# A hybrid decoder block on one core: smaller tiles in the RWKV solve, fewer rows zeroed, another owner of the gating, the dynamic loop moved

## The chip, the cores and the metric

One Trainium2 chip, of which the program uses one core. The metric is the device time of one execution in microseconds (us). The kernel before took 2051.95 us (median of three runs, 2043.92 to 2052.5).

## What is computed

The reference is one decoder layer on 256 tokens of width 2048, in float32:

```python
xn   = rmsnorm(x)
proj = xn @ W_in
attn = moba_attention(proj[..., :A], ...)
rw   = rwkv7_time_mix(token_shift_lerp(proj[..., 3*A:], mu), ...)
h    = x + concat([attn, rw]) @ W_out
h    = h + peer_ffn(rmsnorm(h))
out  = rmsnorm(h, final_g)
```

The attention has 8 heads of 128, all tokens in one block. RWKV has 16 heads of 64, whose state is carried over the tokens. `peer_ffn` scores 128 x 128 product keys for 8 heads, each token keeps the 16 best experts of each head, and the output is the sum over them of `gate * gelu(x . u[e]) * v[e]`, where expert e is one row of `u` and one row of `v` (2048 wide, 16384 rows).

## The kernel before, in words

**Gemms.** Every weight comes in halves of 128x1024 floats (`prefetch`, L191; the load is L197, on SP's queue). ACT rounds a half to a high part (`whi`, L204), DVE subtracts to get the low part (`wlo`, L205), and three matmuls make one product: high x high, high weight x low input, low weight x high input (L218 to L220). In PEER's `gemm_wide` (L234) it is one matmul 512 wide (L240) and one 256 wide (L242) for each of the 16 tiles of the depth; a step of `hidden` is 128 experts, and there are 128 steps.

**Input projection.** `products` (L639) multiplies 8 units of RWKV pairs of heads (r, k, v), then 8 units of attention heads (q, k, v). Each finished unit becomes a generator in `live`; while the next units' matmuls are issued, `deal` and `step_all` step up to four of these generators after every fourth tile. `rwkv` works in 4 chunks of 64 tokens (`NC` = 4). For each chunk it inverts a triangular 64x64 matrix for both heads of the pair at once, as a 128x128 tile with two blocks on the diagonal, in 5 levels of two products (`pw`, L496, and `px`, L502). `clear` (L633) issues the DMAs that zero `rows_d`, a table in HBM with one row of 257 floats per expert: 23 DMAs of 1028 KB (L637), two per pair of RWKV heads and one per attention head until all are issued.

**PEER.** `choose` finds the best 16 keys per tile of 128 tokens, `table` builds the gate table of that tile in HBM (`gate_d`), `hidden` multiplies `u` and takes the gelu on ACT (`gelu`, L1122, from `part`, which DVE adds at L1138). `places` (L1005) gives every chosen expert a row of `rows_d`: first 28 blocks of 128 rows for those that only tile 0 chose, 28 for tile 1 alone, and then a middle part, for those of both tiles and what did not fit before. Experts that nobody chose get a row number past the table, which is written too but never read. `scatter` (L1098) takes step after step of `hidden`: `gated` (L1080) multiplies gate and gelu into an `at` section (on POOL), and an indirect DMA (L1107, issued by POOL) writes its 128 rows to their places. One gate table of 1024 KB (`gt`, L1075, loaded by POOL's queue) serves eight sections, one `at` tile holds seven. `choose`, `table` and `scatter` run beside `hidden`: `run` (L1156) gives each a credit per fourth tile and takes off what each `yield` says that it costs.

**V.** After the last step, blocks of 128 rows of `rows_d` are read back (L1200), the rows of `v` that they name are gathered (an indirect DMA, L1205), split, and multiplied: 28 blocks for tile 0 only, 28 for tile 1 only, `MID` = 52 for both. Reads run five blocks ahead of the matmuls. After all of them, a loop whose count is computed on the chip, `tc.For_i(MID, count)` (L1264), multiplies what the middle part holds beyond 52 blocks. Then the residual is added (L1295), normed, and written (L1286).

With the inputs of the runs the choices need 50.3 blocks of 128 rows in the middle part, worked out from the reference, so `count` is 51: the loop has no iteration, before and after.

```python
        for c in range(NC):
            nc.tensor.matmul(o4(pw)[:, c], M[:, c, 0:128], lo_(X)[:, c], start=(c == 0), ...)
        nc.vector.tensor_tensor(lo_(wm), o4(pw), lo_(lv(i)...), op=ALU.mult)
        yield
```

Of the kernel before, what the change touches and what calls it, by code (L numbers as in the profile page):

```python
# [10 lines left out]
F32 = mybir.dt.float32  # L11
# [51 lines left out]
C0, C1, MID, DN = 28, 28, 52, 2  # L63
B1, BM = C0 * 128, (C0 + C1) * 128
BT = BM + 128 * 128
# [3 lines left out]
def consts():  # L69
# [6 lines left out]
    c[:, K_MSK:K_MSK + P] = same & (p[:, None] < p[None])  # L76
# [3 lines left out]
    for i in range(6):  # L80
        n = 1 << i
        lv = (p[:, None] // (2 * n) == p[None] // (2 * n)) & (p[:, None] % (2 * n) >= n) & (p[None] % (2 * n) < n)
        c[:, K_LV + i * P:K_LV + (i + 1) * P] = lv
        if i == 0:
            c[:, K_M1T:K_M1T + P] = lv.T
# [69 lines left out]
def block_kernel(ctx: ExitStack, tc: tile.TileContext, x, cols, consts, w_lora, w_gate, w_rkv, w_qkv,  # L155
# [13 lines left out]
    rows_d = dp.tile([BT + NEXP, ROW], F32, name="rows_d")  # L169
# [11 lines left out]
    for w, n in ((w_gate, 2), (w_rkv, 3 * RJ), (w_qkv, 3 * AH)):  # L181
        halves += [(w[m, i].rearrange("p k c -> p (k c)"), HK * P) for m in range(n) for i in range(2)]
# [163 lines left out]
    wms = [p1.tile([P, NC, P], F32, name=f"wm{i}") for i in range(1, 6)]  # L346
# [8 lines left out]
    mska = kc(K_MSK, 128).rearrange("p (h t) -> p h t", h=2).unsqueeze(1).to_broadcast([P, 2, 2, CH])  # L355
    mskr = kc(K_MSK + 128, 192).unsqueeze(1).to_broadcast([P, 2, 192])
# [3 lines left out]
    idb = ident.unsqueeze(1).to_broadcast([P, NC, 128])  # L360
# [15 lines left out]
    def rwkv(j, r, k, vv):  # L376
# [82 lines left out]
        for q in range(0, NC, 2):  # L459
            pc = bank("pc", [P, 4, 128])  # L460
            for c in range(2):
                for i, src in enumerate((nbd, kbd)):
                    nc.tensor.matmul(pc[:, 2 * c + i, :], src[:, q + c, :], ar[:, q + c, :],
                                     start=c + i == 0, stop=c + i == 2, skip_group_check=True)
            pc2 = pc.rearrange("p (c i) n -> p c (i n)", c=2)
            nc.vector.tensor_tensor(M[:, q:q + 2, 0:128].rearrange("p a (h t) -> p a h t", h=2),
                                    pc2[:, :, 0:CH].unsqueeze(2).to_broadcast([P, 2, 2, CH]), mska, op=ALU.mult)
            nc.vector.tensor_tensor(M[:, q:q + 2, 128:320], pc2[:, :, CH:], mskr, op=ALU.mult)
            yield

# [13 lines left out]
        for i in range(1, 6):  # L484
            n = 1 << i
            nblk = P // (2 * n)
# [13 lines left out]
            px = bank("px", [P, NC, CH])  # L500
            for c in range(NC):
                nc.tensor.matmul(o4(px)[:, c], wm[:, c, :], hi_(XT)[:, c], start=(c == 0), stop=(c == NC - 1),  # L502
                                 skip_group_check=True)
            nc.vector.tensor_tensor(hi_(XT), hi_(XT), o4(px), op=ALU.add)
            yield

        y = tmp("y", "y")[:, :S]
        Z = None
        for c in range(NC):
# [15 lines left out]
            nc.tensor.matmul(sa_p, XT[:, c, :], r0, start=True, stop=True)  # L525
# [104 lines left out]
    gv = rows_d[0:BT].rearrange("(p f) o -> p f o", p=P)  # L630
    zero = []

    def clear(n):  # L633
        for _ in range(n):
            i = len(zero)
            if i < BT // P // 8:
                zero.append(nc.sync.dma_start(gv[:, 8 * i:8 * i + 8, :], zt.unsqueeze(1).to_broadcast([P, 8, ROW])))  # L637

    def products():  # L639
# [18 lines left out]
        for j in range(RJ):  # L658
            while len(live) > 4:
                step_all()  # L660
# [11 lines left out]
            clear(2)  # L672
        state["pools"] = [spl]
        for h in range(AH):
            while len(live) > 4:
                step_all()
# [8 lines left out]
            clear(1)  # L685

# [236 lines left out]
    def table(t):  # L923


        while t not in chosen:
            yield 0
# [73 lines left out]
    place = cp.tile([P, P], I32, name="place")  # L1001
    eint = sp.tile([P, P], I32, name="eint")
    nblk = cp.tile([P, 1], I32, name="nblk")

    def places():  # L1005
# [12 lines left out]
        off = sp.tile([P, 4], F32, name="off")  # L1018
# [22 lines left out]
        V.scalar_tensor_tensor(pos, mid, -1.0, enum, op0=ALU.mult, op1=ALU.mult)  # L1041
        V.scalar_tensor_tensor(tmp_, mid, -float(BT), pos, op0=ALU.mult, op1=ALU.add)
        V.scalar_tensor_tensor(pos, enum, float(BT), tmp_, op0=ALU.add, op1=ALU.add)
        yield 1.2
        for t, n, base in ((0, C0, 0), (1, C1, B1)):
# [3 lines left out]
            V.scalar_tensor_tensor(tmp_, rank[t], float(base), inside[t], op0=ALU.add, op1=ALU.mult)  # L1049
            V.tensor_tensor(pos, pos, tmp_, op=ALU.add)  # L1050
# [3 lines left out]
        ps = ranks((2, 1))  # L1054
        yield 0.5
        V.tensor_copy(off[:, 2:4], ps[:, :, 0])
        V.scalar_tensor_tensor(rank[2], sums[2], off[:, 2:3], mid, op0=ALU.add, op1=ALU.subtract)
        V.scalar_tensor_tensor(tmp_, rank[2], float(BM), mid, op0=ALU.add, op1=ALU.mult)
        V.tensor_tensor(pos, pos, tmp_, op=ALU.add)
        V.tensor_copy(place, pos)  # L1060

        V.tensor_scalar(off[:, 3:4], off[:, 3:4], 127.0, None, op0=ALU.add)
        V.tensor_copy(nblk, off[:, 3:4])
        V.tensor_scalar(nblk, nblk, 7, None, op0=ALU.logical_shift_right)
        V.tensor_copy(eint, enum)
        chosen["places"] = True
# [13 lines left out]
    def gated(i2, eng=nc.gpsimd):  # L1080

        if i2 % 7 == 0:
            rows[0] = big("at")
            n = min(7, NKEY - i2)
            eng.tensor_copy(rows[0][:, 0:n * ROW].rearrange("p (n c) -> p n c", c=ROW)[:, :, T].bitcast(I32),
                                  eint[:, i2:i2 + n])
# [9 lines left out]
        return at  # L1096

    def scatter():  # L1098
        while "places" not in chosen:
            yield 0  # L1100
        gates_of(0)
        yield 0
        for i2 in range(NKEY - DN):
            while hid["n"] <= i2:
                yield 0
            at = gated(i2)
            s_ = nc.gpsimd.indirect_dma_start(  # L1107
                out=rows_d, out_offset=bass.IndirectOffsetOnAxis(ap=place[:, i2:i2 + 1], axis=0),
                in_=at, in_offset=None)
            for z_ in done:  # L1110
                tc.declare_no_dep(s_.ins, z_.ins, reason="other rows")
            for z_ in zero:
                tc.add_manual_dep(s_.ins, z_.ins.name, SYNC, reason="zeros first")
            done.append(s_)
            yield 1.5
# [38 lines left out]
    beside = [[both_choices(), 0.55, 0.0], [tables(), 0.38, 0.0], [scatter(), 1.0, 0.0]]  # L1154
# [67 lines left out]
    for i2 in range(NKEY - DN, NKEY):  # L1222
        with tc.issue_after(state["gelu"].ins), tc.issue_after(u_end.ins):
            ah, al_ = halves_of(gated(i2, nc.vector)[:, 0:T])
# [18 lines left out]
    for k in range(len(order) + 5):  # L1243
# [18 lines left out]
    count = nc.values_load(nblk[0:1, 0:1], min_val=0, max_val=128,  # L1262
                           skip_runtime_bounds_check_because="a count of at most 16384 experts in blocks of 128")
# [59 lines left out]
```

## Time and profile before

| what | value |
|---|---|
| runs | 2043.92, 2051.95, 2052.5 us |
| profiled execution: its own time / its span | 2048.21 / 2046.3 us |
| PE, DVE, ACT, POOL busy | 95%, 70%, 52%, 35% |
| mean granted TensorE clock | 0.98 |
| DMA | 444 MB, 217 GB/s over the span |

The span runs from the first to the last record; 1.9 us of the execution lie around it. PE is the busiest engine; its row in the 40 slices of the page shows 90% or more everywhere but in the first four slices, the 26th to 28th, the 31st and the last. A busy PE at a granted clock of 1.0 works at 2.4 GHz, at 0.5 at 1.2 GHz.

The names of engines in the rows: PE is TensorE, PEldq its sequencer for weight loads, DVE VectorE, ACT ScalarE, POOL GpSimd, SP SyncE.

### The profile page before, as it was taken

The page shows a single profiled execution, that of the slowest core. Times are in us where ns is not written, and L with a number is a line of the kernel's source. Part 1 is how long each engine was busy: PE and PEld are TensorE (multiplying, and loading weights), DVE is VectorE, ACT ScalarE, POOL GpSimd, SP SyncE. Part 2 cuts the span into 40 slices and gives each one's busy share as a digit, 9 for nine tenths or more (in the row PEclk, how much of TensorE's full clock was granted, in tenths as well). Part 3 has the DMA queues.
Part 4 walks back from the last instruction along what each step waited for, and adds up shares of the span by engine and source line. Part 5 has one row for each costly group of instructions (what it writes and reads, how often), then busy time and mean ns, then how long its engine had stood idle before and what let it go on. Part 6 is the DMA issues. An engine that isn't in the chain of part 4 may idle for free. (4 is left out here: it accounts for less than half of the span.)

```text
span 2046.3 us, 31447 instructions
## 1 busy us (share of the span) xinstructions
PE 1935.7 (95%) x11804; PEld 1723.3 (84%) x11804; DVE 1437.7 (70%) x2090; ACT 1062.9 (52%) x1696; POOL 712.1 (35%) x654
## 2 busy tenths in 40 slices
PE   7888999999999999999999999887998999999996
PEld 6788999999879998878888888776887788888885
DVE  6766878766556888999878866544755666666665
ACT  4534554345455444677676744433444555555554
POOL 7211211100000000023424269998986333333322
PEclk9999999999999999999999999998999999999998
DMA  8999322225576666556666678786888887878783
GB/s 248 258 247 246 98 87 87 88 83 146 190 227 198 184 180 188 173 175 197 215 195 217 196 237 264 248 267 229 270 267 271 343 284 280 296 286 293 281 297 141
DMA packets 135291, 443.91 MB, mean 217 GB/s; under 512 B 14369, under 2 KB 52257, under 8 KB 118497
## 3 DMA queue, kind: packets, MB, share of 16 engines
q1 hardware_dynamic: 106992, 289.24, 47.7%
q0 software_dynamic: 28144, 152.65, 20.4%
q8 instruction: 93, 1.52, 0.3%
q14 instruction: 62, 0.50, 0.1%
HBM read 380.07 MB, written 61.76 MB: 216 GB/s over the span
## 5 line engine op out<-in xcount | busy, mean ns | idle before, releaser
L205 DVE TENSOR_TENSOR wlo<-raw,whi 128x1024 fp32r<-128x1024 f32 (+1 forms) x408 | 569.6, 1402 | 301.1 <-ACT whi L204 291.9
L240 PE MATMUL ps_gm<-nx,whi 128*128 128x512 f32 x2048 | 731.8, 400 | 24.9 <-ACT whi L204 21.9
L204 ACT ACTIVATE whi<-raw 128x1024 fp32r<-128x1024 f32 (+1 forms) x408 | 429.5, 1055 | 384.2 <-issue 89.5
L242 PE MATMUL ps_gm<-nx,wlo 128*128 128x256 f32 x2048 | 579.4, 283 | 14.2 <-DVE wlo L205 14.2
L240 PEld LDWEIGHTS ps_gm<-nx,whi 128*128 128x128 f32 x2048 | 387.8, 189 | 112.6 <-ACT whi L204 22.6
L242 PEld LDWEIGHTS ps_gm<-nx,wlo 128*128 128x128 f32 x2048 | 390.3, 191 | 20.1 <-DVE wlo L205 19.7
L249 DVE TENSOR_TENSOR vlo<-vraw,vhi 128x2048 fp32r<-128x2048 f32 x108 | 247.9, 2297 | 151.6 <-ACT vhi L248 146.1
L248 ACT ACTIVATE vhi<-vraw 128x2048 fp32r<-128x2048 f32 x108 | 205.9, 1913 | 156.3 <-DVE vlo L249 146.8
L1205 POOL DMA_INDIRECT vraw<-in_v_dram,ag x108 | 145.1, 1343 | 294.8 <-PE ps_gm L1194 210.0
L218 PE MATMUL ps_gm<-xh,whi 128*128 128x256 f32 x640 | 192.7, 301 | 0.8 <-ACT whi L204 0.8
L220 PE MATMUL ps_gm<-xh,wlo 128*128 128x256 f32 x640 | 185.1, 289 | 3.2 <-DVE wlo L205 3.1
L219 PE MATMUL ps_gm<-xl,whi 128*128 128x256 f32 x640 | 185.6, 290 | 0.0
L1107 POOL DMA_INDIRECT rows_d<-at,place x126 | 169.5, 1345 | 36.9 <-POOL at L1093 15.8
L951 POOL TENSOR_TENSOR mt<-gc 128x1024 f32<-128x1024 f32 x16 | 39.7, 2482 | 345.5 <-ACT gc L979 345.5
L1122 ACT ACTIVATE A<-part 128x256 f32<-128x256 f32 x128 | 53.1, 415 | 166.7 <-DVE part L1138 131.3
L1093 POOL TENSOR_TENSOR at<-A,gt 128x256 f32<-128x256 f32 x126 | 129.2, 1041 | 5.4 <-DMA gt<-gate_d 3.6
L220 PEld LDWEIGHTS ps_gm<-xh,wlo 128*128 128x128 f32 x640 | 122.8, 192 | 4.6 <-DVE wlo L205 4.2
L218 PEld LDWEIGHTS ps_gm<-xh,whi 128*128 128x128 f32 x640 | 122.9, 192 | 1.9 <-ACT whi L204 1.2
L219 PEld LDWEIGHTS ps_gm<-xl,whi 128*128 128x128 f32 x640 | 122.9, 192 | 0.7
L807 POOL DMA_DIRECT2D skb<-in_sk_dram x16 | 8.6, 540 | 250.7 <-ACT mh L248 167.7
L945 ACT ACTIVATE ob<-ob,pick 128x128 f32<-128x128 f32 x256 | 83.9, 390 | 19.6 <-DVE ob L937 19.6
L373 POOL TENSOR_TENSOR df<-ext 128x256 f32<-128x256 f32 (+1 forms) x28 | 23.8, 850 | 155.3 <-DVE ext L371 142.4
(1521 smaller groups left out, 3925.5 us busy)
## 6 DMA issues: line engine op xcount, KB each, us to landing
raw<-in_u_dram SPq DMA_DIRECT2D x256, 512.0 KB, 4.1
raw<-in_w_rkv_dram SPq DMA_DIRECT2D x48, 512.0 KB, 7.3
raw<-in_w_qkv_dram SPq DMA_DIRECT2D x48, 512.0 KB, 3.6
rows_d<-zt SPq DMA_DIRECT2D x23, 1028.0 KB, 15.8
raw<-in_w_out_dram SPq DMA_DIRECT2D x32, 512.0 KB, 3.9
raw<-in_wq_dram SPq DMA_DIRECT2D x32, 512.0 KB, 3.6
gate_d<-gc SPq DMA_DIRECT2D x16, 1024.0 KB, 6.5
gt<-gate_d POOLq DMA_DIRECT2D x16, 1024.0 KB, 9.0
```

The lines of the kernel that those rows point to most:

```text
L204: nc.scalar.activation(hi[:, :n], raw[:, :n], AF.Copy)
L205: state["dve"] = nc.vector.tensor_tensor(lo[:, :n], raw[:, :n], hi[:, :n].bitcast(F32), op=ALU.subtract)
L218: nc.tensor.matmul(ps, a, xh(kt), start=first and k == 0, stop=False)
L219: nc.tensor.matmul(ps, a, xl(kt), start=False, stop=False)
L220: state["mm"] = nc.tensor.matmul(ps, b, xh(kt), start=False, stop=last and k == HK - 1)
L240: nc.tensor.matmul(ps.rearrange("p z t -> p (z t)"), hi[:, k * P:(k + 1) * P], x_.rearrange("p z t -> p (z t)"), start=i + k == 0, stop=Fa ...
L242: state["mm"] = nc.tensor.matmul(ps[:, 0, :], lo[:, k * P:(k + 1) * P], x_[:, 0, :], start=False, stop=i == 1 and k == HK - 1, skip_group_ ...
L248: nc.scalar.activation(hi, src, AF.Copy)
L249: nc.vector.tensor_tensor(lo, src, hi.bitcast(F32), op=ALU.subtract)
L1093: eng.tensor_tensor(at[:, 0:T].rearrange("p (q t) -> p q t", q=KT), As[i2 // 8][:, k, :].rearrange("p (q t) -> p q t", q=KT), g.rearrange( ...
L1107: s_ = nc.gpsimd.indirect_dma_start(out=rows_d, out_offset=bass.IndirectOffsetOnAxis(ap=place[:, i2:i2 + 1], axis=0), in_=at, in_offset=None)
L1205: nc.gpsimd.indirect_dma_start(out=raw, out_offset=None, in_=vf, in_offset=bass.IndirectOffsetOnAxis(ap=ag[:, T:ROW].bitcast(I32), axis=0))
```

## The change

Six things, in the order of the diff.

1. `MID` 52 to 51; experts that nobody chose get rows behind the middle part, numbered by another rank in `places`; one row tile of zeros is scattered behind them (`behind`, `zr`), so that the last block read of the middle part holds only sound rows. So only the one-tile sections (`BM` rows) are zeroed beforehand: 7 DMAs of 1028 KB in place of 23, one per unit (`clear(1)`).
2. The units are taken in the order r0, r1, r2, a0, r3, a1, ... in place of eight pairs and then eight heads.
3. The solve holds each head's 64x64 matrix by itself: tiles `X`, `XT`, `wm` are half as wide, each product is two matmuls 64x32 per chunk, one per half of the partitions, and one copy per pair (`bd`, on POOL) makes the 128x128 tile that the later product reads.
4. `table` waits until both tiles have chosen; the credits are 0.6 and 0.45 for 0.55 and 0.38.
5. `gated` works on DVE in place of POOL; a section costs the credit 2.0, not 1.5.
6. The loop stands in the sequence of blocks, after step 40, and its blocks end no sum.

```diff
-C0, C1, MID, DN = 28, 28, 52, 2
+C0, C1, MID, DN = 28, 28, 51, 2
-BT = BM + 128 * 128
+BT = BM + (NKEY - DN + 1) * 128
...
+    ORDER = [("r", 0), ("r", 1)] + [x for j in range(2, RJ) for x in (("r", j), ("a", j - 2))] + [("a", AH - 2), ("a", AH - 1)]
...
-            X = W("X", [P, NC, 128], XB)
+            X = W("X", [P, NC, CH], XB)
             nc.vector.transpose(X.rearrange("p c s -> p (c s)"), XT.rearrange("p c s -> p (c s)"))
-            pw = bank("pw", [P, NC, CH])
+            pw = bank("pw", [P, NC, CH // 2])
             for c in range(NC):
-                nc.tensor.matmul(o4(pw)[:, c], M[:, c, 0:128], lo_(X)[:, c], start=(c == 0), stop=(c == NC - 1),
-                                 skip_group_check=True)
+                for hs in both:
+                    nc.tensor.matmul(o4(pw)[hs, c], M[hs, c, 64:128], lo_(X)[hs, c], start=True, stop=True,
+                                     skip_group_check=True)
...
+        XB_ = W("XB", [P, NC, 128], 2)
+        bd(XB_, XT)
...
-            nc.tensor.matmul(sa_p, XT[:, c, :], r0, start=True, stop=True)
+            nc.tensor.matmul(sa_p, XB_[:, c, :], r0, start=True, stop=True)
...
-    gv = rows_d[0:BT].rearrange("(p f) o -> p f o", p=P)
+    gv = rows_d[0:BM].rearrange("(p f) o -> p f o", p=P)
...
-            clear(2)
+            clear(1)
...
-        while t not in chosen:
+        while 0 not in chosen or 1 not in chosen:
...
-    def gated(i2, eng=nc.gpsimd):
+    def gated(i2):
...
-        eng.tensor_tensor(at[:, 0:T].rearrange("p (q t) -> p q t", q=KT),
+        nc.vector.tensor_tensor(at[:, 0:T].rearrange("p (q t) -> p q t", q=KT),
...
+        zr = big("zr")[:, 0:ROW]
+        nc.gpsimd.memset(zr, 0.0)
+        into_rows(zr, behind)
         yield 0
         for i2 in range(NKEY - DN):
             while hid["n"] <= i2:
                 yield 0
             at = gated(i2)
...
-            yield 1.5
+            into_rows(at, place[:, i2:i2 + 1])
+            yield 2.0
...
-    beside = [[both_choices(), 0.55, 0.0], [tables(), 0.38, 0.0], [scatter(), 1.0, 0.0]]
+    beside = [[both_choices(), 0.6, 0.0], [tables(), 0.45, 0.0], [scatter(), 1.0, 0.0]]
...
-    with tc.For_i(MID, count, 1) as i:
-        ag, _ = rows_at(i * P + BM)
-        block((0, 1), *divided(ag, gather(ag)), True)
+        if k == 40:
...
+            with tc.For_i(MID, count, 1) as i:
+                rows[2] = rows[1]
+                ag, _ = rows_at(i * P + BM)
+                rows[1] = rows[2]
+                block((0, 1), *divided(ag, gather(ag)), False)
```

How this moves the instructions is seen at two places. The first is PE's own order in the input projection, around one `pw` product of a solve; gemm is L218 to L220 before and L224 to L226 now, the product L496 and now L502. Before:

```order
L218 MATMUL ps_gm<-xh,whi 128x256
L219 MATMUL ps_gm<-xl,whi 128x256
L220 MATMUL ps_gm<-xh,wlo 128x256
L525 MATMUL ps_ch<-r_1369,XT 128x128
L496 MATMUL ps_pw<-X,M 128x64 x4
L392 MATMUL ps_mm<-lor,l_1377 128x256
L218 MATMUL ps_gm<-xh,whi 128x256
```

Now:

```order
L224 MATMUL ps_gm<-xh,whi 128x256
L225 MATMUL ps_gm<-xl,whi 128x256
L226 MATMUL ps_gm<-xh,wlo 128x256
L557 MATMUL ps_mm<-y,bo_198 128x256
L502 MATMUL ps_pw<-X,M 64x32 x8
L224 MATMUL ps_gm<-xh,whi 128x256
L225 MATMUL ps_gm<-xl,whi 128x256
```

Four products with both heads in one tile became eight with one head each, and each run of eight stands alone between products of 128 rows; there are 80 such runs (8 pairs x 5 levels x 2). In float32 each row of the order is two matmuls in the trace.

The second place is the scatter stage, on POOL, which issues the scatters (`rows_d`) and the loads of the gate tables (`gt`). Before:

```order
L1107 DMA rows_d<-at,place 39936x257 x2
L1075 DMA gt_13178<-gate_d 128x16x128
L1093 TENSOR_TENSOR at<-A_8687,gt_13060 128x256 x2
L1107 DMA rows_d<-at,place 39936x257 x2
L1093 TENSOR_TENSOR at<-A_8687,gt_13060 128x256 x2
L1107 DMA rows_d<-at,place 39936x257 x2
L1093 TENSOR_TENSOR at<-A_8687,gt_13060 128x256
```

POOL now:

```order
L1127 DMA rows_d<-at,place 23424x257 x4
L1103 DMA gt_13934<-gate_d 128x16x128
L1127 DMA rows_d<-at,place 23424x257 x12
L1103 DMA gt_14093<-gate_d 128x16x128
L1127 DMA rows_d<-at,place 23424x257 x8
L1103 DMA gt_14241<-gate_d 128x16x128
```

And DVE now, at the same sections, with the waits of each instruction; `wlo` (L211) is the low half of the weights of `hidden`, `DMASW` a queue of POOL's DMAs:

```order
L211 TENSOR_TENSOR wlo<-raw,whi 128x1024 [waits DMAHW6_49,PE_49,Activation_49]
L1171 TENSOR_TENSOR part<-part,ps_gm 128x256 [waits Activation_49]
L1121 TENSOR_TENSOR at<-A_10407,gt_13934 128x256 [waits DVE_49]
L1121 TENSOR_TENSOR at<-A_10407,gt_13934 128x256 x3
L211 TENSOR_TENSOR wlo<-raw,whi 128x1024 [waits DMAHW7_49,PE_49,Activation_49]
L1121 TENSOR_TENSOR at<-A_10992,gt_14093 128x256 [waits DMASW7_49]
L1121 TENSOR_TENSOR at<-A_10992,gt_14093 128x256
L211 TENSOR_TENSOR wlo<-raw,whi 128x1024 [waits DMAHW0_49,PE_49,Activation_49]
```

The multiplication by the gates has left POOL's order, whose loads of gate tables now stand among the scatters alone; on DVE it stands between the halves of the weights, and its first section of a table waits for that table's load.

## Rows read from the trace of the kernel before

**Rows 1.** Windows: length, then busy us (x) of PE, PEld, DVE, ACT, POOL, clock, DMA, GB/s.

```profile
80.00:205.00 125.00, 109.61 (x855) 106.04 (x854) 88.05 (x163) 51.47 (x88) 23.75 (x39) 0.96 1.03 243
205.00:500.00 295.00, 290.62 (x2344) 281.34 (x2343) 222.02 (x448) 140.80 (x271) 37.26 (x46) 1.00 0.32 95
...
850.00:950.00 100.00, 91.79 (x559) 80.40 (x558) 99.38 (x164) 69.35 (x144) 22.94 (x14) 1.00 0.56 175
...
1230.00:1560.00 330.00, 299.11 (x1665) 257.93 (x1664) 190.97 (x155) 139.32 (x208) 298.07 (x267) 0.96 0.79 257
...
1600.00:2029.00 429.00, 429.00 (x1894) 355.06 (x1892) 274.19 (x210) 231.55 (x208) 137.54 (x101) 1.00 0.78 280
```

**Rows 2.** Waits of ACT, 80 to 200 us: us in total, times, longest.

```profile
ACT whi L204 <- DMA raw<-in_w_rkv_dram: 25.6, 3, 14.1
```

**Rows 3.** DMAs issued, 80 to 200 us: KB each, median us to landing.

```profile
rows_d<-zt SPq DMA_DIRECT2D x16, 1028.0 KB, 16.8
raw<-in_w_rkv_dram SPq DMA_DIRECT2D x21, 512.0 KB, 11.5
```

**Rows 4.** Groups by line and form, PE, 0 to 520 us: busy, mean ns, idle before.

```profile
L496 PE MATMUL ps_pw<-X,M 128*128 128x64 f32 x320 | 40.9, 269 | 1.7 <-DVE X L493 1.6
```

**Rows 5.** Timeline of PE around one product of the solve: start, duration, instruction.

```profile
246.70 1.00 PE L496 MATMUL ps_pw<-X,M 128*128 128x64 f32 x8
247.52 0.36 PE L218 MATMUL ps_gm<-xh,ml 128*128 128x256 f32 x1
247.72 0.28 PE L219 MATMUL ps_gm<-xl,ml 128*128 128x256 f32 x1
247.84 0.28 PE L220 MATMUL ps_gm<-xh,ml 128*128 128x256 f32 x1
```

**Rows 6.** Timeline of PE just after an idle stretch, products two columns wide.

```profile
1201.01 0.58 PE L1033 MATMUL ps_pc<-tot,we 128*128 128x2 f32 x2 [3.50 <-DVE tot L1027]
1201.45 0.57 PE L1034 MATMUL ps_pc<-tot,kb 128*128 128x2 f32 x2
```

**Rows 7.** Windows: the microsecond in which these products start, columns as in rows 1.

```profile
1201.00:1202.00 1.00, 0.99 (x5) 1.00 (x5) 0.49 (x3) 0.00 (x0) 0.29 (x2) 0.50 0.92 295
```

**Rows 8.** Timeline of DVE in the scatter stage.

```profile
1222.47 1.23 DVE L205 TENSOR_TENSOR wlo<-raw,whi 128x1024 fp32r<-128x1024 f32 x1 [1.55 <-ACT whi L204]
1223.61 0.41 DVE L1138 TENSOR_TENSOR part<-part,ps_gm 128x256 f32<-128x256 f32 x1
```

**Rows 9.** Timeline of PE in the V stage, the first of each block's twelve products.

```profile
1996.39 0.39 PE L1192 MATMUL ps_mm<-vhi,ah 128*128 128x512 f32 x1
...
1999.11 0.39 PE L1192 MATMUL ps_mm<-vhi,ah 128*128 128x512 f32 x1
```

**Rows 10.** Waits of ACT, 1200 to 1600 us.

```profile
ACT A L1122 <- POOL at L1093: 30.7, 2, 21.8
```

**Rows 11.** Waits of PE, 1230 to 1560 us.

```profile
PE ps_gm L240 <- ACT whi L204: 21.9, 2, 17.0
```

**Rows 12.** The page's groups of instructions: busy, mean ns, idle before.

```profile
L1107 POOL DMA_INDIRECT rows_d<-at,place x126 | 169.5, 1345 | 36.9 <-POOL at L1093 15.8
...
L1093 POOL TENSOR_TENSOR at<-A,gt 128x256 f32<-128x256 f32 x126 | 129.2, 1041 | 5.4 <-DMA gt<-gate_d 3.6
```

**Rows 13.** Gate loads and gating, 1190 to 1580 us: ns min/median/max; time to landing.

```profile
L1075 POOL DMA_DIRECT2D gt<-gate_d x16: 1167/1203/1235, 1198.5 to 1525.9; - x16
L1093 DVE TENSOR_TENSOR at<-A,gt x2: 621/662/704, 1567.1 to 1572.9; 128x256 f32<-128x256 f32 x2
...
DMA to landing us min/median/max: 6.6/9.0/9.9
```

**Rows 14.** The instructions of the loop's line on PE's sequencer: durations, first and last start.

```profile
L1264 PEldq EVENT_SEMAPHORE  x13: 51/51/51, 2029.2 to 2031.0; - x13
```

**Rows 15.** The chain that ended last, in order of time: start, us, what.

```profile
2029.58 1.88 DVE yr L1295 x3
...
2034.64 0.07 DVE r L1279
```

More of the change, by code (lines that the diff above doesn't have):

```diff
@@ L180, in block_kernel @@
         halves += [(w_lora[m, i].rearrange("p k c -> p (k c)"), HK * LOR) for m in range(2)]
-    for w, n in ((w_gate, 2), (w_rkv, 3 * RJ), (w_qkv, 3 * AH)):
-        halves += [(w[m, i].rearrange("p k c -> p (k c)"), HK * P) for m in range(n) for i in range(2)]
+    ORDER = [("r", 0), ("r", 1)] + [x for j in range(2, RJ) for x in (("r", j), ("a", j - 2))] + [("a", AH - 2), ("a", AH - 1)]
+    blocks_ = [(w_gate, m) for m in range(2)]
+    for what, n in ORDER:
+        blocks_ += [((w_rkv if what == "r" else w_qkv), 3 * n + i) for i in range(3)]
+    halves += [(w[m, i].rearrange("p k c -> p (k c)"), HK * P) for w, m in blocks_ for i in range(2)]
     KP = (4, 5, 6, 7, 0, 1, 2, 3)
@@ L344, in block_kernel @@
     nc.gpsimd.memset(zt, 0.0)
-    wms = [p1.tile([P, NC, P], F32, name=f"wm{i}") for i in range(1, 6)]
+    wms = [p1.tile([P, NC, CH], F32, name=f"wm{i}") for i in range(1, 6)]
     for w in wms:
@@ L657, in products, with pair @@
         state["pools"] = [spl, spl, spare[0]]
-        for j in range(RJ):
-            while len(live) > 4:
-                step_all()
+        def pair(j):
             got = []
@@ L671, in products, with head @@
             live.append(rwkv(j, *got))
-            clear(2)
[L673 to L676, printed above, removed]
+            clear(1)
+        def head(h):
             got = []
@@ L685, in products @@
             clear(1)
+        for k, (what, n) in enumerate(ORDER):
+            while len(live) > 4:
+                step_all()
+            if what == "a":
+                state["pools"] = [spl]
+            yield from (pair if what == "r" else head)(n)
     def step_all(most=4):
@@ L1001, in block_kernel @@
     place = cp.tile([P, P], I32, name="place")
+    behind = cp.tile([P, 1], I32, name="behind")
     eint = sp.tile([P, P], I32, name="eint")
@@ L1017, in places @@
         tot = sp.tile([P, 4], F32, name="tot")
-        off = sp.tile([P, 4], F32, name="off")
+        off = sp.tile([P, 8], F32, name="off")
         for t in range(2):
@@ L1040, in places @@
         V.tensor_tensor(mid, m[0], m[1], op=ALU.max)
-        V.scalar_tensor_tensor(pos, mid, -1.0, enum, op0=ALU.mult, op1=ALU.mult)
-        V.scalar_tensor_tensor(tmp_, mid, -float(BT), pos, op0=ALU.mult, op1=ALU.add)
-        V.scalar_tensor_tensor(pos, enum, float(BT), tmp_, op0=ALU.add, op1=ALU.add)
+        un, sum_u, rank_u = both, m[0], m[1]
+        V.tensor_scalar(un, mid, -1.0, 1.0, op0=ALU.mult, op1=ALU.add)
+        V.memset(un[:, NKEY - DN:], 0.0)
+        V.tensor_tensor_scan(sum_u, ones, un, 0.0, op0=ALU.mult, op1=ALU.add)
+        V.tensor_copy(tot[:, 3:4], sum_u[:, P - 1:P])
         yield 1.2
@@ L1096, in gated, with into_rows @@
         return at
+    def into_rows(src, where):
+        s_ = nc.gpsimd.indirect_dma_start(
+            out=rows_d, out_offset=bass.IndirectOffsetOnAxis(ap=where, axis=0), in_=src, in_offset=None)
+        for z_ in done:
+            tc.declare_no_dep(s_.ins, z_.ins, reason="other rows")
+        for z_ in zero:
+            tc.add_manual_dep(s_.ins, z_.ins.name, SYNC, reason="zeros first")
+        done.append(s_)
     def scatter():
@@ L1106, in scatter @@
             at = gated(i2)
[L1107 to L1115, printed above, removed]
+            into_rows(at, place[:, i2:i2 + 1])
+            yield 2.0
     summed = []
```

70 lines of the change are left out of this document (41 added, 29 removed).

## The prediction

> **What bounds the kernel now.** The page comes first: PE is busy for 95% of the span, the next engine, DVE, for 70%. So this is a PE kernel, and a gain must come from one of three things: stretches in which PE stands still, PE work left out, or the ends of the program. Next I cut the span into stages with the windows [rows 1]. In 205 to 500 us and in 1600 to 2029 us PE lacks next to nothing. It lacks 15.4 us in 80 to 205, 8.2 in 850 to 950 and 30.9 in 1230 to 1560, and in the first and the last of these the granted clock is 0.96, not 1.00. Then I asked of each stretch which wait ends last. In the first it is ACT waiting for the weights' DMA, 25.6 us in three waits [rows 2]; the DMA engines are full there (share 1.03 in rows 1), 16 zeroing DMAs of 1028 KB stand among 21 weight loads of 512 KB on one queue, and a load takes 11.5 us to land [rows 3]. In 850 to 950 DVE is full, 99.38 of 100 us. In 1230 to 1560 PE waits for ACT's rounding, 21.9 us in two waits [rows 11], and ACT for POOL's gating, 30.7 us in two waits [rows 10]: POOL is the full engine, 298 of 330 us [rows 1].
>
> **The sum** is made against the profiled execution, 2048.2 us, which lies 3.7 under the median of the runs.
>
> *Zeros.* Seven DMAs in place of 23: all seven are issued by the 16th or 17th weight half, where the first seven stood before, so up to about 80 us nothing changes and after it the SP queue carries weights alone. The stretch of 80 to 205 us loses 15.4 us idle and, at a clock of 0.96 over 109.6 us of work, 4.4 more [rows 1]. 205 to 500 us, where no zeroing is left, is 1.5% idle; 1.5% of 125 is 1.9. So -15.4 - 4.4 + 1.9 is about -18; I take **-17**, with ends -19.4 (all but nothing left) and -9 (half of the waits belong to loads that would be late anyhow).
>
> *64x64 tiles.* A product of the solve is eight matmuls now, 0.82 us from the first to what follows [rows 5], 0.10 each. The pace isn't set by the 64 columns that stream: with two columns they take 0.22 each [rows 6], at a granted clock of 0.50 [rows 7], twice 0.10 at half the clock. So the weight load sets it. Now there are sixteen per product, each with half the rows and half the columns of weights, and the tile size changes before and after. Low end: the load halves with the columns and the two halves of the array work at once, 16 x 0.05 / 2 = 0.40. High end: no load is shorter and each change refills the array, 16 x 0.10 + 2 x 0.17 = 1.94, where 0.17 is a duration of 0.27 [rows 4] less the spacing of 0.10. I take 0.55, between 0.40 and the 0.80 of half loads one behind the other, plus both refills, 0.34: 0.89 in all, 0.07 more than now. With 80 products in a stage that PE bounds: **+6**, ends (0.40 - 0.82) x 80 = -34 and (1.94 - 0.82) x 80 = +90.
>
> The trace shows no change to a tile of 64 rows, so the 0.17 is an analogy. The Trainium skill has a rule that speaks against this change: TensorEngine Tiling (Array Packing), Key Properties, says that changing the tiling mode drains TensorE, while different tiles may load and multiply in parallel. By its first half the 160 changes cost, by its second the sixteen matmuls get cheap; no run here has shown either. The same skill, TensorE: Matmul & The Clock Gate, section LDWEIGHTS, has the load go with the columns of the weights at a fixed 1.2 GHz; the trace agrees with 0.10 us for 128 columns but shows twice that at the lower clock. By that rule 64 columns take half.
>
> DVE's part of the solve halves (masks, transposes and adds half as wide) and POOL gets one copy per pair: both lie under PE, which waits 1.7 us in all before the products of the first kind [rows 4]; were that cover gone, those 1.7 us would grow, at most to the few us that an operation of POOL takes, once in a pair. **0**. The order of units: the stage after 205 us is full already; **0**.
>
> *Choose and tables.* In 850 to 950 us one tile's table runs beside the other's choice, and DVE lacks room: 8.2 us lost. Now the table waits for both choices, so that overlap goes. But the choice gets 0.6 for 0.55. A step of `hidden` is 16 products 512 wide (2.72 / 12 = 0.227 us each [rows 9]) and 16 of 256 (0.12 [rows 5]): 5.55 us of PE. DVE has its two halves and an addition in a step, 2 x 1.23 + 0.41 = 2.9 [rows 8]; if it is just full now, the choice has 2.6 of it, and 2.6 x 0.6 / 0.55 makes 2.8, so DVE needs 5.7 and each of some twenty steps is 0.15 longer: +3. Together **-5**, ends -8 and +3.
>
> *Scatter stage.* Before it loses 30.9 us idle, and its clock of 0.96 costs an estimated 6: 37. POOL loses 126 gatings of 1041 ns, 131 us [rows 12], so it isn't the bound any more: its scatters alone are 170 us of 330. DVE gets 126 gatings of 0.66 us [rows 13] = 83 us, on 191 of 330. Spread evenly this would fit. But the order bunches them: 21 to 28 sections stand beside four or five steps, so a step with six sections needs 2.9 + 6 x 0.66 = 6.9 us of DVE against PE's 5.55. There are five bunches, 106 sections in 23 steps: 23 x 2.9 + 106 x 0.66 = 137 us of DVE against 23 x 5.55 = 128, so 9 late at least; with seven to nine sections in the fullest steps, the rest being late from inside a bunch, I take 29 before slack. Then the waits: a section that opens a new gate table waits for a load that is queued on POOL behind up to 12 scatters, 12 x 1.65 (1.35 and the 0.30 between them) = 19.8, plus 1.2 to issue and 9.0 to land [rows 13]: 30 us after the start, where DVE has come to it after 20. The five such places make an estimated 30 us, and the next weight half is queued behind each on DVE. The two halves that are ready cover 5.5 us at each of the five, 25 to 28. So 29 + 30 - 26 = 33, and 4 for the clock: 37 again. **0**, ends -37 (DVE keeps up) and +19 (no cover).
>
> *One middle block fewer.* Both its tiles take twelve products, 1999.11 - 1996.39 = 2.72 us each [rows 9], in a stage that is full: **-5.4**.
>
> *The loop at step 40.* It runs no iteration. PE's sequencer is held from 2029.2 to 2031.0 in it now [rows 14]; in mid-stage that is 1.9 us in which PE has nothing. Queued behind it are the gathers of the next blocks; their chain (read, gather, split) refills in an estimated 18 us, against some 16 us of blocks that are ready when the loop begins. **+3**, ends +2 and +6.
>
> *The end.* The residual and the norm of tile 0 (2029.58 to 2034.64 [rows 15]) start after the loop now; with no loop in between they can run beside the five last blocks, which are tile 1's alone, 5 x 2.72 = 13.6 us: **-5**, ends -6 and 0.
>
> Sum: -17 + 6 - 5 + 0 - 5.4 + 3 - 5 = -23.4, so 2048.2 - 23.4 = **2025**.
>
> **Rivals.**
> - *Slower: the solve's small products are dear.* If a load of 64 columns takes as long as one of 128 and each change refills, the term is +90, not +6: 2025 + 84 = 2109. For it speaks that 16 instructions stand where 8 did and that rows 6 show a floor that streaming does not set; against it, that a floor set by the load should fall with its columns. It decides from about 1.3 us a product (0.4 above 0.89, x 80 = 32).
> - *The halves don't overlap.* 0.80 + 0.34 = 1.14 a product, +26 for +6: 2045, about the same as before.
> - *The scatter stage's stall goes.* If DVE's bunches and gate loads hide behind the halves that are ready, -37: 1988. For it: DVE has 139 us free in that stage. Against it: the order, by which weights queue behind waits.
> - *The scatter stage gets worse.* Upper end, +19: 2044.
> - *The loop has an iteration.* If the middle part needed 52 blocks, the block fewer comes back with an uncovered read and gather, an estimated 5.4 + 18: 2048. The choices speak against it.
>
> **How the numbers follow.** Forecast 0.42 (its own range 2005 to 2041), dear products 0.10, no overlap 0.14, stall gone 0.21, scatter worse 0.11, iteration 0.02. Half a per cent, about what a measurement can tell from no change, puts the bounds at 2041.7 and 2062.2. Faster: 0.42 + 0.21 and a part of the two cases near 2045, 0.05: 0.68. Slower: 0.10 and the upper tails of the middle cases, 0.04: 0.14. Same: the rest, 0.18. The range of 1970 to 2056 leaves out the dear products and, below, a stall gone together with the low end of the tiles.
>
> **What would show it.** Right: no wait of ACT for weights over 5 us after 80 us and a clock of 1.00 in the input projection; sixteen small matmuls in 0.4 to 0.7 us, with a gap of about 0.17 on both sides; DVE, not POOL, as the releaser in the scatter stage, with gate loads behind it; a gap of about 2 us of PE at the loop; under 13 us from PE's last product to the end. Wrong: over 1.3 us a product of the solve, or a scatter stage with PE busy throughout.

## The result, and the profile after

The change makes the kernel slower: 2066.71 us (median of seven runs) against 2043.92 (median of seven), a ratio of the means of 1.0099 with an interval of 1.0078 to 1.0121. One run of the changed kernel, 2173.18 us at a granted clock of 0.84, is left out of that ratio. The forecast was 2025, the range 1970 to 2056. The profiled execution has a span of 2063.4 us against 2046.3, 17.1 more.

Where the 17.1 us come from is best read from marks that both traces have: PE's first product of the output projection, its first of `hidden`, DVE's 33rd, 65th, 73rd and last addition into `part` (one in each step of `hidden`), and PE's last product. Times between marks in us:

| stage | before | after | difference |
|---|---|---|---|
| input projection, from 0 | 540.7 | 509.4 | -31.3 |
| output projection and queries | 195.2 | 197.6 | +2.4 |
| steps 0 to 31 of `hidden` | 209.4 | 191.3 | -18.1 |
| steps 32 to 63 | 220.0 | 236.6 | +16.6 |
| steps 64 to 71 | 58.4 | 65.8 | +7.4 |
| steps 72 to 127 (scatters) | 348.4 | 402.1 | +53.7 |
| V stage | 456.8 | 448.5 | -8.3 |
| from PE's last product | 17.5 | 12.1 | -5.4 |

So the input projection, the first 32 steps, the V stage and the end brought more than forecast, and the later steps, above all those beside the scatters, gave it all back. The windows of after, with the columns of [rows 1], show the same. The stretch of 80 to 205 us has gone from 109.6 us of PE to 122.3, at a granted clock of 1.00, with 0.41 of the DMA engines for 1.03. 850 to 950 is full. 950 to 1190 lacks 14.8 us, where the kernel before lacked none. 1230 to 1560, which lacked 30.9 us of PE, lacks 72.1, at a clock of 0.88.

```profile
80.00:205.00 125.00, 122.33 (x1224) 114.44 (x1223) 93.43 (x182) 59.50 (x100) 25.51 (x38) 1.00 0.41 121
205.00:500.00 295.00, 288.82 (x2851) 270.56 (x2850) 207.69 (x430) 148.00 (x272) 42.52 (x55) 1.00 0.34 110
...
850.00:950.00 100.00, 100.00 (x617) 88.83 (x616) 88.89 (x101) 72.38 (x156) 21.85 (x14) 1.00 0.59 192
950.00:1190.00 240.00, 225.25 (x1382) 200.13 (x1381) 191.02 (x211) 160.01 (x355) 97.73 (x66) 0.97 0.59 199
...
1230.00:1560.00 330.00, 257.89 (x1382) 221.35 (x1383) 182.37 (x251) 116.69 (x174) 186.51 (x123) 0.88 0.71 228
...
1600.00:2029.00 429.00, 421.42 (x1849) 347.54 (x1848) 273.58 (x210) 234.69 (x212) 147.61 (x107) 1.00 0.81 297
```

Which wait ends last in that stage? PE's waits of after in 1230 to 1560 us answer to [rows 11]: not ACT's rounding any more, but DVE.

```profile
PE ps_gm L246 <- DVE part L1171: 42.5, 7, 20.2
PE ps_gm L248 <- DVE wlo L211: 30.0, 6, 13.3
```

And DVE's waits in the same stretch say what holds DVE: the load of the gate table (73 of 73 + 72 + 7 us; the 72 are short waits for the rounding, which any step has).

```profile
DVE at L1121 <- DMA gt<-gate_d: 73.1, 5, 20.4
DVE wlo L211 <- ACT whi L210: 71.8, 52, 5.8
DVE at L1121 <- ACT A L1155: 6.6, 14, 0.5
```

The longest of the five shows how it comes about. First DVE's timeline of after, from a series of gatings (`at`) to the end of the wait:

```profile
1264.09 2.46 DVE L1121 TENSOR_TENSOR at<-A,gt 128x256 f32<-128x256 f32 x4
...
1270.63 0.40 DVE L1171 TENSOR_TENSOR part<-part,ps_gm 128x256 f32<-128x256 f32 x1
...
1277.94 0.40 DVE L1171 TENSOR_TENSOR part<-part,ps_gm 128x256 f32<-128x256 f32 x1
1278.27 2.42 DVE L1121 TENSOR_TENSOR at<-A,gt 128x256 f32<-128x256 f32 x4
1280.62 1.21 DVE L211 TENSOR_TENSOR wlo<-raw,whi 128x1024 fp32r<-128x1024 f32 x1
1302.18 1.15 DVE L1121 TENSOR_TENSOR at<-A,gt 128x256 f32<-128x256 f32 x2 [20.36 <-DMA gt<-gate_d]
1303.24 1.22 DVE L211 TENSOR_TENSOR wlo<-raw,whi 128x1024 fp32r<-128x1024 f32 x1
```

POOL's timeline of after in the same time:

```profile
1265.07 6.52 POOL L1127 DMA_INDIRECT rows_d<-at,place  x1 [15.87 <-DVE at L1121]
1271.89 6.96 POOL L1127 DMA_INDIRECT rows_d<-at,place  x1 [0.30 <-issue]
1279.16 3.51 POOL L1127 DMA_INDIRECT rows_d<-at,place  x1 [0.30 <-DVE at L1121]
1282.97 0.97 POOL L1127 DMA_INDIRECT rows_d<-at,place  x1 [0.30 <-issue]
...
1293.17 0.97 POOL L1127 DMA_INDIRECT rows_d<-at,place  x1 [0.31 <-DMA rows_d<-at,place]
1294.14 1.20 POOL L1103 DMA_DIRECT2D gt<-gate_d  x1
```

While DVE gates, two scatters take 6.5 and 7.0 us; as soon as DVE stands still they take 0.97. What lets a long one go can be read from the same rows: the two end at 1271.59 and 1278.85, 0.96 and 0.92 us behind the start of an addition into `part`, which reads one input from PSUM (`ps_gm`), while the gatings and the low halves around it read both from SBUF. Of the 13 scatters of after that take over 2.1 us, nine end 0.92 to 1.00 us behind the start of such an addition, two end 0.84 and 0.85 behind DVE's falling idle, and two 0.96 and 0.99 behind the start of a small copy (L1113).

So the twelve scatters that stand ahead of the load in POOL's order need 29.1 us (1265.07 to 1294.14), and the table lands some 8 us later. DVE had come to it at 1281.8. Behind DVE's wait stand the low half of the weights (1303.24) and the addition, and PE is without work:

```profile
1304.85 0.80 PE L246 MATMUL ps_gm<-nx,whi 128*128 128x512 f32 x1 [20.16 <-DVE part L1171]
```

The granted clock falls with the wait too: it is 0.59 on average in the 20.16 us without work and 0.69 in the 6.15 us of work behind them. For all of the stage the windows give, first before:

```profile
1224.00:1572.00 348.00, 313.27 (x1746) 270.17 (x1744) 201.32 (x168) 147.81 (x220) 307.97 (x275) 0.96 0.79 257
```

and after:

```profile
1201.00:1603.00 402.00, 323.74 (x1750) 277.95 (x1748) 229.35 (x329) 147.75 (x220) 214.89 (x143) 0.90 0.71 225
```

PE stands still for 78.3 us against 34.7, which is 43.5 of the 54; the other 10.5 are the same products taking longer (323.7 for 313.3 us) at a clock of 0.90 for 0.96. POOL, the full engine of before, is busy for 215 of 402 us, and DVE for 229: no engine is full any more, and the stage is longer.

### The profile page after: what moved, and what is told of

Same layout as the page of the kernel before. It is cut to its first block, busy times and chain, and to the rows that moved or that the text cites. A ratio compares the mean times of both kernels' runs of the same rounds, so it can differ in the third digit from the quotient of the medians.

```text
span 2063.4 us, 32573 instructions
## 1 busy us (share of the span) xinstructions
PE 1925.3 (93%) x12420; PEld 1697.6 (82%) x12420; DVE 1439.6 (70%) x2225; ACT 1065.5 (52%) x1700; POOL 613.3 (30%) x519
## 5 line engine op out<-in xcount | busy, mean ns | idle before, releaser
L211 DVE TENSOR_TENSOR wlo<-raw,whi 128x1024 fp32r<-128x1024 f32 (+1 forms) x418 | 526.4, 1262 | 239.6 <-ACT whi L210 238.7
L1127 POOL DMA_INDIRECT rows_d<-at,place x126 | 194.6, 1544 | 174.3 <-DVE at L1121 144.4
L224 PE MATMUL ps_gm<-xh,whi 128*128 128x256 f32 x720 | 220.5, 306 | 2.6 <-ACT whi L210 2.6
L226 PE MATMUL ps_gm<-xh,wlo 128*128 128x256 f32 x720 | 206.2, 287 | 2.4 <-DVE wlo L211 2.4
L225 PE MATMUL ps_gm<-xl,whi 128*128 128x256 f32 x720 | 206.5, 287 | 0.0
L224 PEld LDWEIGHTS ps_gm<-xh,whi 128*128 128x128 f32 x720 | 137.7, 191 | 6.3 <-ACT whi L210 3.4
L226 PEld LDWEIGHTS ps_gm<-xh,wlo 128*128 128x128 f32 x720 | 137.7, 191 | 4.2 <-DVE wlo L211 3.8
L1121 DVE TENSOR_TENSOR at<-A,gt 128x256 f32<-128x256 f32 x128 | 79.5, 668 | 87.8 <-DMA gt<-gate_d 77.4
L225 PEld LDWEIGHTS ps_gm<-xl,whi 128*128 128x128 f32 x720 | 138.0, 192 | 0.9
L950 DVE TENSOR_TENSOR ob<-iota,pick 128x512 f32<-128x512 f32 x64 | 72.7, 1135 | 3.2 <-POOL act L970 3.2
L224 PE MATMUL ps_gm<-yh,whi 128*128 128x256 f32 x256 | 73.5, 288 | 0.0
```

The lines of the kernel that those rows point to most:

```text
L211: state["dve"] = nc.vector.tensor_tensor(lo[:, :n], raw[:, :n], hi[:, :n].bitcast(F32), op=ALU.subtract)
L224: nc.tensor.matmul(ps, a, xh(kt), start=first and k == 0, stop=False)
L225: nc.tensor.matmul(ps, a, xl(kt), start=False, stop=False)
L226: state["mm"] = nc.tensor.matmul(ps, b, xh(kt), start=False, stop=last and k == HK - 1)
L1127: s_ = nc.gpsimd.indirect_dma_start(out=rows_d, out_offset=bass.IndirectOffsetOnAxis(ap=where, axis=0), in_=src, in_offset=None)
```

## The experiments

The theory after the result: DVE's gating stands in order behind gate tables whose loads are queued on POOL behind the scatters. Rivals: DVE's added work in bunches by itself; `places`, which ends later in the steps than before, and the one more scatter. A further question is which part of the change made the gains.

The kernel before was run again beside each of these kernels: its median was 2046.4 to 2047.8 us, for 2043.9 beside the changed kernel, which was not run again. So a time here less the changed kernel's 2066.7 is sure to some 4 us.

### Gating back on POOL

```diff
-    def gated(i2):
+    def gated(i2, eng=nc.gpsimd):
...
-        nc.vector.tensor_tensor(at[:, 0:T].rearrange("p (q t) -> p q t", q=KT),
+        eng.tensor_tensor(at[:, 0:T].rearrange("p (q t) -> p q t", q=KT),
...
-            yield 2.0
+            yield 1.5
```

> The changed kernel with its gating back on POOL (and the section's cost back at 1.5). Theory: the 97 us that the scatter stage (from the 73rd step of hidden to the last) loses now come from DVE standing in order behind gate tables, so the stage goes back from 402 us to about the 348 of before and the time to about 2012 us. Rival (the later places and one more scatter do it, whoever gates): the stage stays above 380 us and the time above 2045.

2033.48 us, a ratio to the kernel before of 0.9921 (0.9897 to 0.9945). Steps 72 to 127 take 368.4 us: below the rival's 380 but 20 above what the theory wanted. The stage is POOL's again, by ACT's waits of this kernel in it:

```profile
ACT A L1155 <- POOL at L1121: 18.2, 2, 14.8
ACT A L1155 <- DMA rows_d<-at,place: 14.4, 1, 14.4
```

So moving the gating to DVE cost 33.7 us in this stage and 33.2 in the time (2066.7 - 2033.5), and not all of what the stage lost. For the other 20 us the rival has a share: the first scatter starts 9.1 us behind the 73rd addition, where it started 3.8 ahead of it before, which makes 13. From the first scatter to the last are 351.6 us for 343.6, which makes some 8; why that grew was not separated.

### Gate tables loaded from SP's queue

```diff
-            nc.gpsimd.dma_start(gts[g], gate_d[:, :, g * P:(g + 1) * P])
+            nc.sync.dma_start(gts[g], gate_d[:, :, g * P:(g + 1) * P])
```

> The changed kernel with DVE's gating kept, the gate tables loaded from SP's queue instead of POOL's, so that no scatter stands ahead of them. Theory (it is the loads queued behind the scatters, 77 us of DVE's waits): DVE's waits for gt fall under 15 us and the time to 2015 to 2030 us. Rival (it is DVE's added work in bunches): no more than 10 us gained, 2055 us or more. A second rival: SP now waits for the table's buffer and holds up the weights behind it, seen as ACT waiting for u by far more than 43 us.

1996.8 us, 0.9758 (0.9728 to 0.9789): one line is worth 70 us, more than the theory gave, and the version beats both kernels. Steps 72 to 127 take 333.5 us. DVE's wait for `gt` in the stage has gone from 73 us to 6:

```profile
DVE at L1121 <- DMA gt<-gate_d: 5.8, 3, 2.6
```

and the window of the stage has PE idle for 20.0 us at a clock of 0.98, with DVE's 231 us of work unchanged:

```profile
1200.00:1534.00 334.00, 313.99 (x1752) 270.54 (x1751) 231.25 (x330) 149.46 (x220) 203.54 (x128) 0.98 0.88 275
```

Both rivals fall: DVE's work in bunches costs at most these 20.0 us of idle PE, and SP isn't held up (ACT waited 42 us for u in the stretch of 1190 to 1570). The scatters are as long as in the changed kernel, a mean of 1.60 us for 1.54, and one of them is the longest of all runs, beside gatings; now no load waits behind them:

```profile
1214.80 9.01 POOL L1127 DMA_INDIRECT rows_d<-at,place  x1 [0.30 <-DVE at L1121]
```

### Both: gating on POOL, gate tables loaded from SP

The diff is that of the last two together, the credit of 1.5 included.

> The changed kernel with both: gating on POOL as before, gate tables loaded from SP. Theory (POOL is the full engine where it gates, 298 of 330 us; the place of the loads matters only where DVE gates): about e1_gating_on_pool, 2025 to 2033, steps 72 to 127 in 360 to 368 us. Rival (the loads' place alone was the loss, whoever gates): 2005 or less. The longest scatters stay near 2 us here, against 9 us where DVE gates.

2017.19 us, 0.9861 (0.9839 to 0.9882), between theory and rival: the place of the loads is worth 16 us even where POOL gates, against 70 where DVE does. In the four kernels the stage of steps 72 to 127 and the time are:

| gating / gate loads | POOL's queue | SP's queue |
|---|---|---|
| on POOL | 368.4, 2033.5 us | 351.6, 2017.2 us |
| on DVE | 402.1, 2066.7 us | 333.5, 1996.8 us |

With the loads on POOL, the move of the gating costs 33 us; with the loads on SP it is worth 20. The 20 rests on the times, whose runs don't overlap (2014.44 to 2023.72 and 1991.94 to 2003.21). The stage of 333.5 us is that of one execution; three further kernels below with DVE's gating and SP's loads take 329.7, 349.1 and 350.3 in theirs. The change had the right idea and one load in the wrong queue.

### Gate tables two ahead, still from POOL

```diff
-            gts[g] = big(f"gt{g % 2}").rearrange("p (q t) -> p q t", q=KT)
+            gts[g] = big(f"gt{g % 3}").rearrange("p (q t) -> p q t", q=KT)
...
             gates_of(i2 // 8 + 1)
+            gates_of(i2 // 8 + 2)
...
         gates_of(0)
+        gates_of(1)
```

> The changed kernel with DVE's gating and POOL's loads kept, each gate table loaded one table (eight sections) earlier in POOL's order. Theory (a load is late because of what stands ahead of it in POOL's order, not because POOL issues it): DVE's waits for gt fall from 77 us to under 20 and the time to 1995 to 2015 us. Rival (POOL falls behind DVE by more than eight sections in a bunch, since its scatters take up to 7 us beside DVE's series of gatings): 40 us of waits or more are left and the time stays above 2030.

2024.58 us, 0.9888 (0.9856 to 0.9919). The waits fall as the theory says, to one of 17.4 us:

```profile
DVE at L1122 <- DMA gt<-gate_d: 17.4, 1, 17.4
```

but the time lies between theory and rival, and the stage takes 361.9 us. So the position in POOL's order, with the third buffer that it needs, explains 42 of the 70 us (2066.7 - 2024.6). What the SP queue has beyond that, 28 us, lies partly in this last wait; the rest was not separated.

### All rows zeroed

```diff
-    gv = rows_d[0:BM].rearrange("(p f) o -> p f o", p=P)
+    gv = rows_d[0:BT - BT % 1024].rearrange("(p f) o -> p f o", p=P)
...
-            clear(1)
+            clear(2)
```

with 22 DMAs in place of 7.

> The changed kernel with 22 zeroing DMAs, issued two with a pair of RWKV heads and one with an attention head, in place of 7. Theory: the zeros were worth about 18 us of the 31 that the input projection gained, so the projection ends 15 to 20 us later and the time is 2081 to 2087 us, all of it before 205 us. Rival (the gain of the projection is the smaller tiles'): under 8 us.

2072.61 us, 5.9 more than the changed kernel, the projection ending at 519.4 in place of 509.4. So the zeros are worth 10 us there, between theory and rival; by the time alone, 5.9, it would be the rival's. 80 to 205 us:

```profile
80.00:205.00 125.00, 115.75 (x1141) 108.44 (x1141) 85.46 (x166) 55.54 (x94) 25.10 (x37) 0.99 0.97 239
```

That is 6.6 us less of PE than in the changed kernel at 0.97 of the DMA engines; the kernel before, with 1.03, had 12.7 less [rows 1]. A reason may be that behind the zeros stand the weights of pairs and heads in turn here, not those of pairs alone; that was not tested.

### The solve with 128x128 tiles

The masks, `XT`, `X`, `wm` and the two products as before, no copy to `XB_`:

```diff
-                for hs in both:
-                    nc.tensor.matmul(o4(pw)[hs, c], M[hs, c, 64:128], lo_(X)[hs, c], start=True, stop=True,
-                                     skip_group_check=True)
+                nc.tensor.matmul(o4(pw)[:, c], M[:, c, 0:128], lo_(X)[:, c], start=(c == 0), stop=(c == NC - 1),
+                                 skip_group_check=True)
```

> The changed kernel with the 128x128 tiles of the solve back. Theory: eight products took 0.82 us and the next 0.08 more than usual, sixteen take 0.58 and 0.10, so 80 of them are worth 9 to 18 us, and the time is 2075 to 2085 us, the projection ending that much later. Rival (PE has slack there, or the change of tile size costs elsewhere): within 5 us of the changed kernel, or faster.

2077.4 us, 10.7 more than the changed kernel; the projection ends at 523.6 for 509.4, 14.2 later. The tiles are a gain, as the timeline of after shows at one product:

```profile
203.17 0.28 PE L226 MATMUL ps_gm<-xh,wlo 128*128 128x256 f32 x1
203.38 0.66 PE L502 MATMUL ps_pw<-X,M 64*64 64x32 f32 x16
203.97 0.39 PE L224 MATMUL ps_gm<-xh,whi 128*128 128x256 f32 x1
204.19 0.28 PE L225 MATMUL ps_gm<-xl,whi 128*128 128x256 f32 x1
204.31 0.28 PE L226 MATMUL ps_gm<-xh,wlo 128*128 128x256 f32 x1
```

Sixteen start within 203.38 to 203.97: 0.59 us for 0.82 [rows 5], 0.037 each. Around them the spacing is 0.21 before and 0.22 behind where 0.12 is usual, some 0.19 in all; the large tiles had 0.08 behind, without any change of size [rows 5]. On PE 80 x (0.82 + 0.08 - 0.59 - 0.19) is 10 us; the other 4 weren't pinned.

### The old order of units, the old tables, the loop at the end

These three stand on the kernel with SP's loads (1996.8 us), each with one part undone.

```diff
-    ORDER = [("r", 0), ("r", 1)] + [x for j in range(2, RJ) for x in (("r", j), ("a", j - 2))] + [("a", AH - 2), ("a", AH - 1)]
+    ORDER = [("r", j) for j in range(RJ)] + [("a", j) for j in range(AH)]
```

> The kernel of e2_gate_loads_on_sp (1996.8 us) with the units back in the order of before, eight pairs and then eight heads. Theory (of the 31 us that the projection gained, e3 and e4 explain 10 and 14, so the order has the rest): the projection ends 5 to 9 us later, near 517 us, time 2002 to 2007. Rival (the parts overlap and the order is worth nothing, as forecast): within 3 us.

2002.95 us. The projection ends at 516.1 for 510.7, 5.4 later, inside the theory's range; the stage behind it is 2.2 shorter (195.1 for 197.3), so 3 us of the order are left, and its runs (1996.15 to 2010.84) overlap those of the kernel with SP's loads (1991.94 to 2003.21).

```diff
-        while 0 not in chosen or 1 not in chosen:
+        while t not in chosen:
...
-    beside = [[both_choices(), 0.6, 0.0], [tables(), 0.45, 0.0], [scatter(), 1.0, 0.0]]
+    beside = [[both_choices(), 0.55, 0.0], [tables(), 0.38, 0.0], [scatter(), 1.0, 0.0]]
```

> The kernel of e2_gate_loads_on_sp with the tables and choices as before (a table waits for its own tile's choice alone, rates 0.55 and 0.38). Theory: the 18 us that steps 0 to 31 gained come back in steps 32 to 71 as 24 us, since the table's work on PE is only moved; so undoing it gives 488 us for steps 0 to 71 for 492, and 1988 to 1996 in all. Rival: the later part's loss is from the longer places, and undoing the rates costs 10 us or more (2007).

1996.15 us (1984.77 to 2003.61), at the theory's upper end. Steps 0 to 71 take 209.8 + 220.0 + 57.3 = 487.1 us, as in the kernel before, for 191.9 + 236.5 + 63.7 = 492.1. So this part of the change moves 18 us and costs 5. In the medians that doesn't show: the scatter stage took 349.1 us in this execution and 333.5 in that of the kernel with SP's loads, though both have the same scatters: PE is busy there for 326 us at a granted clock of 0.96, for 314 at 0.98. The times of either kernel spread over 11 to 19 us.

```diff
-        if k == 40:
-
-            count = nc.values_load(...)
-            with tc.For_i(MID, count, 1) as i:
...
+    count = nc.values_load(...)
+    with tc.For_i(MID, count, 1) as i:
```

> The kernel of e2_gate_loads_on_sp with the loop after all blocks again. Theory: PE loses 2 to 4 us at the loop in mid-stage, and tile 0's closing beside the last blocks gives 5 to 8: so 2000 to 2003 us, the blocks ending 2 to 4 us earlier and the tail being 5 to 8 longer. Rival (the tail is set by the output's writes): 1993 or less.

2003.65 us (1994.2 to 2012.96), just above the theory's upper end, with runs that overlap those of the kernel with SP's loads. The V stage takes 446.0 us for 447.7, and the end 16.6 for 9.2: the loop costs 1.7 us in mid-stage and gives 7.4 back. PE's waits of the changed kernel in the V stage show its price there as one entry of 2.0, which ends at 1773.97:

```profile
PE ps_mm L1225 <- issue: 2.0, 1, 2.0
```

### A third of the gating on POOL

On the kernel with SP's loads and the old tables:

```diff
-        nc.vector.tensor_tensor(at[:, 0:T].rearrange("p (q t) -> p q t", q=KT),
+        eng = nc.gpsimd if i2 % 3 == 2 and i2 < NKEY - DN else nc.vector
+        eng.tensor_tensor(at[:, 0:T].rearrange("p (q t) -> p q t", q=KT),
```

> The kernel of e6_sp_old_tables (1996.15 us: gate tables loaded from SP, tables and choices as before) with every third section's gating on POOL. Theory (what is left in steps 72 to 127, 330 to 350 us against 305 of PE's own work, is DVE's bunches): DVE loses 28 us of work, the stage comes to 320 to 335 us and the time to 1975 to 1990. Rival (POOL's gating holds up its scatters, and DVE's series are only broken by waits for POOL): 1996 or more.

1995.68 us, 0.976 (0.9733 to 0.9786): no gain on 1996.15, and 0.3 us under the rival's 1996. Steps 72 to 127 take 333.7 us, at the theory's edge, in an execution of 1992.5 us; the 349.1 of the kernel that it stands on come from one of 2003.6, so the two stages can't be compared. The longest scatter is 3.24 us here.

## Why the prediction was wrong, point by point

**The scatter stage** is the step that failed: forecast 0, ends -37 and +19, measured +53.7. The mechanism was named: a section that opens a table waits for a load behind up to twelve scatters, with the weights queued behind it on DVE. Two terms of its sum were mis-sized.
- *The wait.* "The five such places make an estimated 30 us": they make 77.4 us in six waits over all of the gating (73.1 in five of them above), a mean of 14.6 in the five where the step had 6. The step priced a scatter at 1.65 us from the kernel before, where POOL gated. Beside DVE's series of gatings it takes up to 7.1 us. In the example above, from the first scatter to the table's use are 37 us where the step had 30, and DVE arrives after 16.7 where it had 20: the wait is 20.4 us for the 10 that the step's own figures give behind twelve scatters.
- *The cover.* "The two halves that are ready cover 5.5 us at each of the five": they didn't. In the example DVE waits 20.36 us and PE 20.16. The low half and the addition that PE needs next both stand on DVE behind the wait, so nothing was ready but the 2.9 us that PE had begun. In sum PE waited 72.5 us for DVE in 1230 to 1560 us, where DVE waited 73.1 for tables. Not all of it is the tables': over the whole stage PE waits 75.9 us for DVE, and 15.5 are left with SP's loads, where DVE's waits for tables have gone from 77.4 to 5.8. So of 72 us of such waits 60 had reached PE.

The rival "the stall goes" comes nearest with another queue for the loads: that kernel loses 28 us against the 305 of PE's own work (55 steps at 5.55), where the changed kernel loses 97 and the kernel before 43. So its stage gains 15, not the rival's 37. The other term of the step, 29 us for the bunches before any slack, has the right size beside the 20.0 us of idle PE that this kernel still has.

**Choice and tables**, forecast -5, cost 5. The 8.2 us of idle PE in the overlap did go, and with 10 us of PE's work moved out of them steps 0 to 31 gain 18.1. But steps 32 to 71 give 24 us back, which the step didn't have: it looked at the stretch in which the overlap costs and not at where the table's work goes. Of the 24, 12.7 are work of PE, the 10 that moved among them, and 11.3 are new idle time. Two waits of after, for ACT in the table and for DVE in `places`, have 10.3 of the 14.8 us that PE stands still in these steps; the second was 3.5 us before [rows 6]:

```profile
PE ps_pw L982 <- ACT gc L992: 5.8, 2, 3.5
PE ps_pc L1047 <- DVE tot L1041: 4.5, 1, 4.5
```

**Zeros**: -17 forecast, -10 measured in the projection (-6 in the time), near the end of -9. **Tiles**: +6 forecast, -14 measured in the projection (-11 in the time). The sixteen products took 0.59 us, near the 0.55 taken; but the refills came to 0.19 in place of 0.34, and the 0.08 that the large tiles had already was not taken off. **Order**: 0 forecast, some 3 to 5 us gained. **The block fewer, the loop, the end**: -5.4, +3 and -5 forecast, -8.3 and -5.4 measured in the V stage and at the end, that is -13.7 for -7.4; part of the V stage's rest lies in its start, where in the first 40 us PE stands still for 3.4 us in place of 5.6, at a granted clock of 0.96 in place of 0.83. With DVE gating the V stage took 447.7 us and with POOL's 454.0, both with loads from SP.

Of the chances, "dear products" had 0.10 for the slower side; slower it was, but by the middle rival (the stage gets worse, 0.11), at nearly three times its upper end. Four of the signs named for being right came true all the same: sixteen products in 0.4 to 0.7 us, DVE with gate loads behind it as the releaser in the scatter stage, about 2 us of PE at the loop, and under 13 us from PE's last product to the end. They point at the mechanism and say nothing of its size.

A rule that was not weighed: the Trainium skill, SBUF — State Buffer, in SBUF: two separate sides, says that DVE and GpSimd share a pair of ports under an exclusive lock, which an operation of DVE takes in a two-port mode, or with two inputs from SBUF against an operation of GpSimd that reads SBUF. It adds that GpSimd cannot write the descriptors of its own DMAs while DVE holds the lock in a two-port mode, and advises to issue the DMA from SP or ACT. The traces agree with it in direction: the longest scatter is 2.04 us where POOL gates, 3.24 where a third is on POOL, and 9.01 where DVE does it all, and nine of the 13 long ones of after end just behind the start of an operation with one input in SBUF. Which of the two cases this would be, and that the lock is the cause, is argued from this; no run changed it alone.

## What to carry to other kernels

When work moves to another engine, look at what it will wait for there, in whose queue that stands, and what is queued behind the wait on the new engine; a cover counts only if it doesn't pass through the waiting engine. A duration taken from rows in which another engine did the work gives no upper end: the 1.65 us a scatter were up to 7.1 beside DVE's work. And a change of several parts should be read stage by stage: here 63 us of gains and 80 of losses made +17.

## What the runs showed of the hardware that was not expected

- An indirect DMA's issue on POOL took 0.97 us beside an idle DVE and up to 9.01 beside a series of DVE's operations with both inputs in SBUF (0.67 us a multiplication); it ended some 0.95 us behind the start of an addition that reads PSUM (nine of 13 of after, and the 9.01 too, which ends 0.92 behind one). Where POOL gates it never took more than 2.04.
- Products of 64x32 that alternate between the two halves of the array start 0.037 us apart, where 128x64 took 0.10; a run of them had about 0.1 us of extra spacing on either side, of which the large tiles had 0.08 behind already.
- The same load of 1024 KB, issued from SP in place of POOL, made 70 us of difference, though the kernel issues it only sixteen times.
